# Four shifts of buffers and issue points in a two-layer streaming encoder: inputs loaded into query buffers, mixture stores, value differences and factor casts issued later

## The chip, the cores and the metric

The kernel runs on one core of one Trainium2 chip. The time is the device time of one execution in microseconds; the median of several executions is what counts. The engines are named as the profile names them: PE multiplies matrices (PEld loads its weights beside it), DVE, ACT and POOL work element by element, and SP issues nearly all DMAs, one after the other, in one queue.

## The reference, cut to what matters

One sequence of 2048 frames with 1024 channels goes through two layers, in float32.

```python
# layer 0: pooling mixer, then a gated embedding
h = rms_norm(x, a_norm);  u, z = split(h @ w_in, 2)
pooled = trailing_means(u, windows 2, 4, 8, 16) - u
x = x + (group_linear(pooled) * scale * silu(z)) @ w_out
x = x + (p[0] @ ple_w[0]) * sigmoid(x @ ple_gate_w[0])
# shared keys and values
k, v = split(rms_norm(x, kv_norm) @ w_kv, 2);  k = rms_norm(k by head, k_norm)
# layer 1: stick-breaking attention, 16 heads of 64
q, z = split(rms_norm(x, b_norm) @ w_in, 2);  q = rms_norm(q by head, b_q_norm)
a[t, s] = sigmoid(l[t, s]) * prod over s < j < t of (1 - sigmoid(l[t, j]))
x = x + ((a @ v) * silu(z)) @ w_out
x = x + (p[1] @ ple_w[1]) * sigmoid(x @ ple_gate_w[1])
```

## The kernel before

**Numbers in two parts.** Every float32 operand of PE is split into a rounded high part and the rest, its low part: ACT casts the high part, then DVE (or POOL) subtracts it from the source (`split`, L187 and L188 to L189; for weights `put_split`, L208 and L210 without a gain, L214 and L215 with one). A product takes three matmuls: high by high, high by low, low by high.

**Stages.** The sequence is cut into four chunks of 512 frames. `opening` runs layer 0 of chunk 0 (`mixed_part(0)`, `gated_part(0)`) and of chunk 1, and then `pair_part(0, 1)`, which makes keys, values, queries and gates of both chunks. `attend` then runs the attention of chunks 0 and 1, with the matmuls of layer 0 of chunks 2 and 3 interleaved (`beside_first`). `middle` does the gates of chunk 3 and `pair_part(2, 3)`; a second `attend` runs the attention of chunks 2 and 3 beside the end of layer 1; the last chunk's end comes alone.

**The pair.** `pair_part` multiplies a 2 by 2 block of activations (two chunks by two halves of the channels) with a 2 by 2 block of weights in seven products instead of eight (p1 to p7, 48 matmuls each, for each of the kinds v, k, q, z in the first pair and v, k, q in the second). The activation factors of p3 to p7 are differences, made by `build` on DVE and split; the weight factors of p4 to p7 are differences as well, made by `mixtures`: four weight tiles are loaded (L950), scaled by ACT (L970), subtracted by DVE (L976), and stored in `mixed`. The mixtures of k, q and v are made beside `gated_part(0)` and `mixed_part(1)`, one step every nine matmuls; those of z inside the first pair from its matmul 480 on, one step every six. `evacuate` takes the results out of PSUM (L993 on DVE, L997 on ACT) and hands them on; values go to `valued`, which makes a copy shifted by one frame by DMA (L752, L756) and has `differences` subtract it (L762), copy the high part (L765), make the low part (L766) and store both.

**Time inside the program.** A counter advances by one with every matmul. `after(n, do)` traces `do` n matmuls later and `store(n, ...)` a DMA to memory n matmuls later (L70). What is traced is then laid out by a scheduler with a simulated timeline of its own (`schedule_with_timeline_sim=True`): an instruction may stand earlier in its engine's queue than where it was traced, when its inputs are ready on that timeline, except where `tc.keep_in_program_order` pins it behind the instruction traced before it on its engine. In the pairs all matmuls are pinned; the loads of `mixtures` (L950) are pinned, and the loads of x in `prep` (L543) are pinned outside the attention.

**Buffers.** Raw weights (L225), x (L543), residuals and a few others share the ring `io` of four buffers; taking a buffer first settles the split of the tile that was there. The queries of the attention have the tag `q`, four buffers, which also hold the x of chunk 0 at the start (`load_first`) and, in the pairs, two split factors: the last one of p2 and the first one of p6 (`home`). `prep(1)` runs beside `gated_part(0)`, one tile of x every 22 matmuls; `prep(2)` in the last 140 matmuls of the first pair, one tile every 10; `prep(3)` beside the first attention. x is cast and split, and squared (L449, L452) for the norm; after the last reader its buffer is free.

**Weights** are planned in one list (`plan`); `pump` keeps up to nine units ahead of PE, and a unit is given back when its matmuls are done.

Of the kernel before, what the change touches and what calls it, by code (L numbers as in the profile page):

```python
# [10 lines left out]
F32 = mybir.dt.float32  # L11
F32R = mybir.dt.float32r
AF = mybir.ActivationFunctionType
ALU = mybir.AluOpType
# [18 lines left out]
def f(ap):  # L33
    return ap.bitcast(F32)


def half_of(pr, l):
    return pr[l] if isinstance(pr, tuple) else pr[:, l]
# [3 lines left out]
def trunk_kernel(ctx, tc, x, p, a_norm, wu_t, wz_a, w_group, a_scale, a_w_out, kv_norm, w_kv,  # L42
                 k_norm, b_norm, b_w_q, b_w_z, b_w_zs, b_q_norm, b_w_out, ple_a, ple_b, gate_a, gate_b, out):
    nc = tc.nc
    V, A, G = nc.vector, nc.scalar, nc.gpsimd
# [19 lines left out]
    def after(n, do):  # L65
        heapq.heappush(waiting, (time["now"] + n, time["seq"], do))
        time["seq"] += 1

    def store(n, **k):
        after(n, lambda: nc.sync.dma_start(**k))  # L70

    def late(n, *todo):

        def do():
            for op in todo:
                tc.keep_in_program_order(op())

        after(n, do)

    def pass_time(n=1):  # L80
        time["now"] += n
        while waiting and waiting[0][0] <= time["now"]:
            heapq.heappop(waiting)[2]()
# [44 lines left out]
    def scratch(name, shape):  # L128
        return dram.tile(shape, F32, name=name)
# [6 lines left out]
    vd = [[scratch(f"vd{s}_{b}", [8, P, 4, P]) for b in range(2)] for s in range(NSUB)]  # L136
# [5 lines left out]
    def flat(tag, bufs, dt=F32):  # L142
        return lambda nm, dt=dt: pool.tile([P, W5], dt, tag=tag, name=nm, bufs=bufs)
# [4 lines left out]
    def io(nm, owner=None):  # L148
        if ring[0] is not None:
            settle(ring[0])  # L150
        ring.append(owner)
        return io_(nm)
# [6 lines left out]
    qryt = flat("q", 4, F32R)  # L159
# [27 lines left out]
    def split(pr, src, lo, n=0):  # L187
        high = lambda: A.copy(out=half_of(pr, 0), in_=src)  # L188
        low = lambda: lo.tensor_tensor(out=half_of(pr, 1), in0=src, in1=f(half_of(pr, 0)), op=ALU.subtract)  # L189
        if n and not state["solo"]:  # L190
            late(n, high, low)
        else:
            high()
            low()
# [61 lines left out]
    def settle(pr):  # L256
        finish = unsplit.pop(id(pr), None)
        if finish:
            finish()
# [13 lines left out]
    def give_back():  # L273
# [10 lines left out]
    mixed = {(kind, name): scratch(f"mixed{kind}{name}", [P, 4, W5]) for kind in KINDS for name in PRODUCTS  # L284
             if name not in WHOLE and (kind != KINDS[0] or name not in READY)}
# [251 lines left out]
    def prep(s):  # L537
        ck = chunk[s]
        ck["x"] = []
        for o in range(KT):  # L540
            pr = pair("xp") if o < 7 else (row("xh", F32R), row("xl", F32R))
            xin = io("xin", pr)
            ins = nc.sync.dma_start(out=xin, in_=x[o * P : (o + 1) * P, s * W5 : (s + 1) * W5])  # L543
            ck["x"].append(pr)

            def finish(o=o, pr=pr, xin=xin):
                split(pr, xin, V if state["hold"] and state["solo"] else G)
                gather_squares(ck, "acc1", o, xin)

            if state["solo"]:  # L550
                tc.keep_in_program_order(ins)
            unsplit[id(pr)] = finish
            after(12 if state["solo"] else 20, lambda pr=pr: settle(pr))
            yield
        if not state["hold"]:
            pass_time(12)
            ck["rb1"] = bcast(token_norm(ck["acc1"], "x"), "x")
            return

        def total():  # L560
            ck["r1"] = token_norm(ck["acc1"], "x")

        def spread():
            ck["rb1"] = bcast(ck["r1"], "x")

        lag.append((time["now"] + 36, total))
        lag.append((time["now"] + 48, spread))
# [177 lines left out]
    def valued(s, b, j, vr):  # L745
        vs = tmp("vs")
        r0 = s * W5 + j * P
        store(6, out=vraw[b][r0 + P - 1 : r0 + P], in_=vr[P - 1 : P])

        def shifted():  # L750
            if r0:
                nc.sync.dma_start(out=vs[0:1], in_=vraw[b][r0 - 1 : r0])  # L752
            else:
                V.memset(vs[0:1], 0.0)
            for lo, hi in ((0, 112), (112, P - 1)):
                nc.sync.dma_start(out=vs[lo + 1 : hi + 1], in_=vr[lo:hi])  # L756

        after(10, shifted)
        after(38, lambda: differences(s, b, j, vr, vs))

    def differences(s, b, j, vr, vs):
        V.tensor_tensor(out=vs, in0=vs, in1=vr, op=ALU.subtract)  # L762
        vs = vs.rearrange("q (h d) -> q h d", d=HD)
        vv = t4("vv").rearrange("q l (h d) -> q (l h d)", d=HD).rearrange("q (h l d) -> q h l d", l=2, d=HD)
        after(4, lambda: A.copy(out=vv[:, :, 0, :], in_=vs))  # L765
        after(8, lambda: V.tensor_tensor(out=vv[:, :, 1, :], in0=vs, in1=f(vv[:, :, 0, :]), op=ALU.subtract))  # L766
        store(16, out=vd[s][b][:, :, j, :].rearrange("h q n -> q h n"),
              in_=f(vv).rearrange("q h e d -> q h (e d)"))

    def keyed(s, kind, b, j, qs):  # L770
# [110 lines left out]
    sets = {}  # L881
# [28 lines left out]
    def build(s):  # L910
        a11, a12 = sets["raw"][:4], sets["raw"][4:]
        rows, rb = chunk[s].pop("rows"), chunk[s]["rb2"]
        sets.pop("raw")
        for name in ("p3", "p5", "p7", "p6", "p4"):
            sets[name] = [home(8 + i) if name == "p6" and i < 3 else pair("xs") for i in range(4)]
        for i in range(4):
            V.tensor_tensor(out=rows[i][:, 1], in0=rows[i][:, 1], in1=rb, op=ALU.mult)
            split(sets["p5"][i], rows[i][:, 1], V)
        yield
        for i in range(4):  # L920
            V.tensor_tensor(out=rows[i][:, 0], in0=rows[i][:, 0], in1=rb, op=ALU.mult)
            V.tensor_tensor(out=rows[i][:, 0], in0=a11[i], in1=rows[i][:, 0], op=ALU.subtract)
            split(sets["p7"][i], rows[i][:, 0], V)
            yield
            V.tensor_tensor(out=a11[i], in0=rows[i][:, 1], in1=a11[i], op=ALU.subtract)
            split(sets["p6"][i], a11[i], V)
            yield
        for i in range(4):
            V.tensor_tensor(out=a12[i], in0=a12[i], in1=a11[i], op=ALU.subtract)
            split(sets["p3"][i], a12[i], V)  # L930
            yield
        for i in range(4):
            raw, scale = scaled(s, 4 + i, tmp)
            yield
            scale()
            split(sets["p4"][i], raw, V)
            yield

    def spare(n):
# [3 lines left out]
    def mixtures(kinds):  # L943
        todo = [(kind, i) for kind in kinds for i in range(4)]

        def load(kind, i):
            src, b0 = SOURCES[kind][0], 2 if kind == "v" else 0
            w = [spare(n) if kind == "z" else ppt("mx") for n in range(4)]
            for n, t in enumerate(w):
                tc.keep_in_program_order(nc.sync.dma_start(out=t, in_=src[b0 + n % 2][:, i + n // 2 * 4]))  # L950
            return w

        def put(kind, name, i, t):
            if kind == KINDS[0] and name in READY:
                pr = t4("mv")
                split(pr, t, V)
                d = once[kind, name, i] = scratch(f"mv{name}{i}", [P, 2, 1, W5])
                store(12, out=d.rearrange("q l k n -> q l (k n)"), in_=f(pr))
            else:
                store(12, out=mixed[kind, name][:, i], in_=t)  # L960

        w = None
        for n, (kind, i) in enumerate(todo):
            if w is None:
                w = load(kind, i)
                for _ in range(8):
                    yield
            for m, t in enumerate(w):
                kt = i + m // 2 * 4
                A.activation(out=t, in_=t, func=AF.Identity, scale=SOURCES[kind][1][:, kt : kt + 1])  # L970
            yield
            b11, b12, b21, b22 = w
            w = None
            for m, (name, a, b, c) in enumerate((("p5", b11, b12, b11), ("p7", b12, b22, b12),
                                                 ("p6", b22, b22, b11), ("p4", b21, b21, b22))):
                V.tensor_tensor(out=a, in0=b, in1=c, op=ALU.subtract)  # L976
                put(kind, name, i, a)
                if m == 0 and kind != "z" and n + 1 < len(todo):
                    w = load(*todo[n + 1])
                yield  # L980
            yield
            yield
# [458 lines left out]
```

## Time and profile before

| | us |
|---|---|
| median of three executions | 2677.32 |
| lowest and highest | 2673.27, 2681.02 |
| the profiled execution | 2670.83 |
| its span on the core | 2668.7 |
| granted share of PE's clock | 0.995 |

The profile is of one execution that is 6.5 us faster than the median. Idle time and waits below are taken from it. A row of waits gives who waited, for whom, the total in us, how often, and the longest one; a row of a window gives its bounds and length, the busy time of PE, PEld, DVE, ACT and POOL with their counts of instructions, the granted share of PE's clock, the busy share of the DMA engines and what they moved in GB/s. "SPq" is the DMA queue of SP.

### The profile page before, as it was taken

How to read it: one execution, taken by the hardware profiler on the slowest of the kernel's cores; microseconds unless marked ns; L12 is line 12 of the kernel's file. 1: busy time of each engine (PE TensorE's matmuls, PEld its weight loads, DVE VectorE, ACT ScalarE, POOL GpSimd, SP SyncE). 2: the span in 40 equal slices, each digit the busy share in tenths (PEclk: the TensorE clock that was granted, in tenths of full speed). 3: DMA queues.
4: the chain of work that ended last, by engine and by line, in shares of the span. 5: the costliest groups of instructions: out<-in, count | busy, mean ns of one | idle time of the engine just before them, and what ended most of it. 6: DMA issues, size and time to landing. Idle time of an engine off the chain costs nothing.

```text
span 2668.7 us, 38357 instructions
## 1 busy us (share of the span) xinstructions
PE 2620.7 (98%) x13070; PEld 2186.1 (82%) x13070; DVE 2035.1 (76%) x2812; ACT 1465.8 (55%) x2900; POOL 572.0 (21%) x470
## 2 busy tenths in 40 slices
PE   9999999999999999999999999999999999999999
PEld 7887888787788888888887888888888888888887
DVE  6746658776568887798677766889898999999842
ACT  5334335465557766555444675666665665556521
POOL 1214321143224325332310433110000100010000
PEclk9999999999999999999999999999999999999999
DMA  6799998877877898677868568765755574556554
GB/s 250 262 336 332 357 351 270 248 243 226 285 271 272 314 313 281 235 260 244 296 214 259 173 209 292 258 203 182 245 174 182 175 244 159 193 179 228 165 199 151
DMA packets 319551, 649.16 MB, mean 243 GB/s; under 512 B 48222, under 2 KB 87134, under 8 KB 319356
## 3 DMA queue, kind: packets, MB, share of 16 engines
q1 hardware_dynamic: 318780, 645.92, 71.7%
q8 instruction: 103, 1.69, 0.3%
q10 hardware_dynamic: 576, 0.79, 0.1%
q14 instruction: 92, 0.75, 0.1%
HBM read 464.66 MB, written 173.60 MB: 239 GB/s over the span
## 4 chain that ended last, share of the span: by engine, by line
PE 73%; DVE 12%; DMA 6%; ACT 3%; issue 3%; SPq 2%; POOL 1%; DVEq 0%; ACTq 0%; POOLq 0%
PE psd L51 38%; PE pso L51 8%; PE psl L51 8%; PE psa L55 7%; PE total L51 6%; PE own L51 5%; DVE pp L1231 3%; DVE at L1251 2%; DMA xin<-in_x_dram 1%; SPq L70 1%; POOL rq L181 1%; DMA vs<-qs 1%; DVE wpair L210 1%; PE pst L55 1%; DVE us L595 1%
## 5 line engine op out<-in xcount | busy, mean ns | idle before, releaser
L1231 DVE TENSOR_TENSOR_SCAN pp<-pp,floor 128x512 f32<-128x512 f32 (+3 forms) x640 | 725.3, 1169 | 10.8 <-ACT pp L1227 10.6
L1249 ACT CAST at<-psa 128x512 fp32r<-128x512 f32 (+3 forms) x640 | 302.5, 524 | 356.0 <-PE psa L55 354.2
L51 PE MATMUL psd<-x,wpair 128*128 128x512 f32 x1920 | 472.9, 391 | 0.0
L1251 DVE TENSOR_TENSOR at<-psa,at 128x512 fp32r<-128x512 f32 (+3 forms) x640 | 358.9, 599 | 122.6 <-ACT at L1249 120.2
L51 PEld LDWEIGHTS psd<-x,wpair 128*128 128x128 f32 x1920 | 358.8, 188 | 75.7 <-DMA wpair<-once 0.4
L51 PE MATMUL psd<-xp,wpair 128*128 128x512 f32 x1392 | 338.7, 392 | 0.3 <-DVE wpair L215 0.2
L51 PE MATMUL pso<-at,vv 128*128 128x512 f32 (+3 forms) x1280 | 318.9, 367 | 11.4 <-DVE at L1251 11.1
L1227 ACT ACTIVATE pp<-psl 128x512 f32<-128x512 f32 (+3 forms) x640 | 312.5, 549 | 7.5 <-PE psl L51 6.7
L51 PEld LDWEIGHTS psd<-xp,wpair 128*128 128x128 f32 x1392 | 258.5, 188 | 55.6 <-DVE wpair L215 1.1
L55 PE MATMUL psa<-ident,pp 128*128 128x128 f32 x2176 | 291.8, 274 | 0.0
L51 PEld LDWEIGHTS pso<-at,vv 128*128 128x128 f32 x1280 | 229.8, 188 | 72.3 <-DVE at L1251 26.8
L51 PE MATMUL total<-wpair,xs 128*128 128x512 f32 x1152 | 276.7, 396 | 6.3 <-DVE qs L993 4.1
L55 PEld LDWEIGHTS psa<-ident,pp 128*128 128x128 f32 x2176 | 252.9, 141 | 27.6
L51 PEld LDWEIGHTS total<-wpair,xs 128*128 128x128 f32 x1152 | 215.8, 189 | 53.6 <-DVE qs L993 4.5
L51 PE MATMUL psl<-kk,qa 128*128 128x512 f32 (+3 forms) x640 | 257.6, 407 | 0.0
L51 PE MATMUL psl<-kk,qb 128*128 128x512 f32 (+3 forms) x640 | 233.1, 364 | 2.4 <-ACT qb L1194 2.4
L51 PE MATMUL own<-wpair,xs 128*128 128x512 f32 x864 | 208.0, 396 | 4.8 <-ACT wpair L214 2.0
L51 PEld LDWEIGHTS own<-wpair,xs 128*128 128x128 f32 x864 | 161.5, 190 | 40.0 <-DVE wpair L215 2.8
L1279 POOL TENSOR_TENSOR os<-os,zt 128x512 f32<-128x512 f32 x32 | 52.2, 1632 | 638.9 <-ACT os L1278 618.8
L51 PE MATMUL psd<-og,wpair 128*128 128x512 f32 x744 | 185.2, 390 | 0.0
L51 PE MATMUL psd<-mp,wpair 128*128 128x512 f32 x768 | 179.9, 390 | 0.0
L51 PEld LDWEIGHTS psd<-mp,wpair 128*128 128x128 f32 x768 | 143.4, 188 | 29.9
(154 smaller groups left out, 3515.6 us busy)
## 6 DMA issues: line engine op xcount, KB each, us to landing
wpair<-once SPq DMA_DIRECT2D x322, 512.0 KB
kk<-kd SPq DMA_DIRECT2D x160, 256.0 KB
vv<-vd SPq DMA_DIRECT2D x160, 256.0 KB
once<-wpair SPq DMA_DIRECT2D x52, 512.0 KB
wpair<-wf SPq DMA_DIRECT2D x48, 512.0 KB
once<-kp SPq DMA_DIRECT2D x40, 512.0 KB
vd<-vv SPq DMA_DIRECT2D x32, 512.0 KB
kd<-hl SPq DMA_DIRECT2D x64, 256.0 KB
```

What stands on the lines that cost most here:

```text
L51: return held_in_order(nc.tensor.matmul(*a, **k))
L55: return held_in_order(nc.tensor.transpose(*a, **k))
L70: after(n, lambda: nc.sync.dma_start(**k))
L181: G.tensor_tensor(out=out_ap, in0=ms, in1=neghalf[:, 0:w], op=ALU.pow)
L210: (G if state["lo"] % state["every"] == 0 else V).tensor_tensor(out=pr[:, 1], in0=raw, in1=f(pr[:, 0]), op=ALU.subtract)
L595: V.tensor_tensor(out=us[:, lo:][:, ::-1], in0=cur[:, lo:][:, ::-1], in1=cur[:, lo - sh : n][:, ::-1], op=ALU.add)
L1227: A.activation(out=pp[:, r0:], in_=ps[:, :w], func=AF.Sigmoid, scale=-1.0)
L1231: V.tensor_tensor_scan(out=pp[:, r0:][:, ::-1], data0=pp[:, r0:][:, ::-1], data1=least, initial=1.0 if st["diag"] else st["carry"][j], op0 ...
L1249: A.copy(out=at[:, 0, cs], in_=pt[:, cs])
L1251: return lambda: V.tensor_tensor(out=at[:, 1, cs], in0=pt[:, cs], in1=f(at[:, 0, cs]), op=ALU.subtract)
L1279: G.tensor_tensor(out=os, in0=os, in1=zt, op=ALU.mult)
```

## The change

Five places are touched. In `prep` the tiles of x of chunks 1 and 2 are loaded into the four query buffers instead of the ring `io`, which also drops the settling of a ring tile there. Value differences are traced 44 instead of 38 matmuls behind their DMAs' start, their high copy 11 instead of 4 behind that, the low part 15 instead of 8, and the store 23 instead of 16. In `build` the split of every difference is traced five or six matmuls after the difference instead of at once. In `mixtures` the stores of the z mixtures are traced 20 instead of 12 matmuls behind, and the wait between the first loads and their use is 11 steps instead of 8.

```diff
@@ prep
-            xin = io("xin", pr)
+            xin = qryt("xin", F32) if s < 3 else io("xin", pr)
@@ valued
-        after(38, lambda: differences(s, b, j, vr, vs))
+        after(44, lambda: differences(s, b, j, vr, vs))
@@ differences
-        after(4, lambda: A.copy(out=vv[:, :, 0, :], in_=vs))
-        after(8, lambda: V.tensor_tensor(out=vv[:, :, 1, :], in0=vs, in1=f(vv[:, :, 0, :]), op=ALU.subtract))
-        store(16, out=vd[s][b][:, :, j, :].rearrange("h q n -> q h n"),
+        after(11, lambda: A.copy(out=vv[:, :, 0, :], in_=vs))
+        after(15, lambda: V.tensor_tensor(out=vv[:, :, 1, :], in0=vs, in1=f(vv[:, :, 0, :]), op=ALU.subtract))
+        store(23, out=vd[s][b][:, :, j, :].rearrange("h q n -> q h n"),
@@ build
-            split(sets["p5"][i], rows[i][:, 1], V)
+            after(6, lambda i=i: split(sets["p5"][i], rows[i][:, 1], V))
...
-            split(sets["p7"][i], rows[i][:, 0], V)
+            after(5, lambda i=i: split(sets["p7"][i], rows[i][:, 0], V))
...
-            split(sets["p6"][i], a11[i], V)
+            after(5, lambda i=i: split(sets["p6"][i], a11[i], V))
...
-            split(sets["p3"][i], a12[i], V)
+            after(5, lambda i=i: split(sets["p3"][i], a12[i], V))
...
-            split(sets["p4"][i], raw, V)
+            after(5, lambda i=i, raw=raw: split(sets["p4"][i], raw, V))
@@ mixtures
-                store(12, out=mixed[kind, name][:, i], in_=t)
+                store(20 if kind == "z" else 12, out=mixed[kind, name][:, i], in_=t)
...
-                for _ in range(8):
+                for _ in range(11):
                     yield
```

## The prediction

> **What bounds the kernel now.** First the head of the page, then the windows of the stages (first start to attention of chunks 0 and 1, that attention, gates and second pair, the second attention), then the chain that ended last.
>
> ```profile
> span 2668.7 us, 38357 instructions
> ```
>
> ```profile
> 8.00:785.00 777.00, 755.38 (x3476) 622.41 (x3477) 517.37 (x791) 377.30 (x673) 203.82 (x181) 0.99 0.84 288
> 785.00:1290.00 505.00, 499.18 (x2618) 421.41 (x2617) 426.24 (x572) 321.31 (x703) 174.75 (x140) 1.00 0.79 272
> 1290.00:1640.00 350.00, 346.56 (x1583) 284.76 (x1582) 233.92 (x351) 187.19 (x329) 102.55 (x88) 1.00 0.73 235
> 1640.00:2560.00 920.00, 910.28 (x4933) 769.73 (x4932) 830.30 (x1021) 561.40 (x1166) 82.15 (x51) 1.00 0.60 199
> ```
>
> ```profile
> 469.85 10.88 PE own L51 x48
> ```
>
> PE is the bound everywhere. Where it runs undisturbed it takes 10.88 / 48 = 0.227 us a matmul of 512 columns, and the change neither adds nor removes a matmul. So only PE's idle time can move: 777.0 - 755.4 = 21.6 us in the first row, where all five edits act, and 350.0 - 346.6 = 3.4 us in the third, where those in `differences` and `build` act again. To this comes PE time at a lowered clock behind the longer stalls. The waits of PE, asked window by window, say where it is (beside `gated_part(0)`; in the first pair around 515, 624 and 731 us; in the second pair):
>
> ```profile
> PE psd L51 <- DVE wpair L210: 2.9, 2, 2.1
> PE psd L51 <- ACT wpair L208: 2.2, 1, 2.2
> ```
>
> ```profile
> PE own L51 <- ACT wpair L214: 1.1, 1, 1.1
> PE own L51 <- DVE wpair L215: 0.7, 1, 0.7
> ```
>
> ```profile
> PE total L51 <- DVE qs L993: 4.1, 1, 4.1
> ```
>
> ```profile
> PE own L51 <- DVE qs L993: 2.8, 1, 2.8
> ```
>
> ```profile
> PE own L51 <- ACT qs L997: 1.2, 1, 1.2
> PE own L51 <- DVE wpair L215: 0.9, 1, 0.9
> PE own L51 <- ACT wpair L214: 0.9, 1, 0.9
> ```
>
> The windows around the three largest, with the granted clock in the column after POOL:
>
> ```profile
> 210.00:240.00 30.00, 24.89 (x105) 19.67 (x104) 21.16 (x22) 12.55 (x22) 14.93 (x10) 0.94 0.94 322
> 600.00:640.00 40.00, 34.03 (x150) 27.12 (x149) 25.45 (x41) 22.87 (x42) 11.61 (x10) 0.91 0.83 260
> 690.00:740.00 50.00, 45.69 (x199) 36.73 (x198) 23.39 (x37) 24.97 (x43) 0.00 (x0) 0.93 0.89 282
> ```
>
> The clock adds 0.06 x 30 = 1.8, 0.09 x 40 = 3.6 and 0.07 x 50 = 3.5 us to them.
>
> **How much a later trace point moves.** Four of the five edits only trace an instruction some matmuls later. Whether it moves on the chip is seen from two that the edits' kin made before:
>
> ```profile
> 425.94 0.48 DVE L754 MEMSET vs<- 1x512 f32 x1
> ```
>
> ```profile
> 437.05 1.29 PE L51 MATMUL own<-wpair,xs 128*128 128x512 f32 x5
> ```
>
> ```profile
> 544.78 0.69 DVE L976 TENSOR_TENSOR mz<-mz 128x512 f32<-128x512 f32 x1 [4.67 <-ACT mz L970]
> ```
>
> ```profile
> 545.50 0.32 SPq L70 DMA_DIRECT2D mixedzp<-mz  x1
> ```
>
> The memset of the first value tile is traced some 70 matmuls into the pair, yet it runs 11 us before p2, matmul 48, begins. The first z mixture's store, traced 12 matmuls (2.7 us) behind its subtraction, is issued 0.03 us after it. So a delay moves only what competes for a busy engine, and what is pinned. A pinned load traced later does go later.
>
> **The change part by part.**
>
> *x in query buffers, chunk 1.* Nothing is added: eight loads, casts, subtractions and squares as before. The raw gate weights get the ring `io` to themselves. SP's waits from 180 to 230 us show what the sharing cost:
>
> ```profile
> SPq L225 <- POOL xp L189: 2.5, 3, 0.8
> SPq L225 <- ACT sq L452: 2.0, 1, 2.0
> SPq L225 <- ACT acc L449: 0.5, 1, 0.5
> ```
>
> SP stood 5.0 us before raw weights because readers of x held the buffer, and what is behind stands too. PE then waits for the last weights of a group, the embedding's:
>
> ```profile
> 224.87 0.72 PE L51 MATMUL psd<-ple,wpair 128*128 128x512 f32 x2 [2.16 <-ACT wpair L208]
> ...
> 228.35 2.08 PE L51 MATMUL psd<-ple,wpair 128*128 128x512 f32 x4 [2.05 <-DVE wpair L210]
> ```
>
> With those 5.0 us back the weights come before they are needed: -(2.16 + 2.05 + 1.8) = -6.0. Bounds: 0, if the DMA engines are full anyway, and -6.9 with the first wait (2.9 - 2.05 = 0.9), which I leave since its weight stood in DVE's queue. The query buffers cannot be late here: a tile every 22 matmuls over four buffers leaves each 88 x 0.227 = 20 us.
>
> The Trainium skill says on its page "TensorE: Matmul & The Clock Gate", section "What's actually happening", that the clock halves after at least one idle window of about 3.4 us. Here two idle stretches of 2.2 and 2.1 us, with three matmuls between, stand beside a granted 0.94, so the row decides; by the page this term would be -4.2 and the sum below -7.8.
>
> *x in query buffers, chunk 2.* The same at the end of the first pair, but at one tile per 10 matmuls. PE has no wait there, so 0; what it can cost is the third case below.
>
> *z mixtures.* The stores stay where they are (the rows above). The wait of 11 steps for 8 moves the pinned loads of the next items: from matmuls 480, 570, 660, 750 to 480, 588, 696, 804. The fourth made the 4.1 us stall:
>
> ```profile
> 612.03 3.24 SPq L950 DMA_DIRECT2D mz<-in_b_w_z_dram  x4
> ```
>
> ```profile
> 617.62 0.72 ACT L970 ACTIVATE mz<-mz,gains 128x512 f32<-128x512 f32 x1 [5.67 <-DMA mz<-in_b_w_z_dram]
> ```
>
> ```profile
>   DMA mz<-in_b_w_z_dram: 15.9, 6
> ```
>
> ```profile
> PE pst L55 <- DVE qs L993: 0.9, 1, 0.9
> ```
>
> ACT stood 5.67 us on this load, with the squares, key casts and copies out of PSUM behind it, DVE behind those, and PE behind L993. There are six such waits (15.9 us of idle time before L970); the others cost PE at most the 0.9 us of the last row, at 547 us. 54 matmuls (12.2 us) later it falls between p6 and p3 of the queries, where DVE alone empties p3's banks. Ends: -(4.1 + 3.6) = -7.7 if it hurts nowhere, +7.7 if it hurts again and one of the two others moved does as well. I take half the gain, -3.9.
>
> *Mixtures of k, q, v.* The first wait shifts the chain by 3 x 9 matmuls, 6.1 us. Its end passes the end of `mixed_part(1)`, where the rest is run at once; those weights are used a whole `gated_part` later. 0, between -0.9 and +0.9, the first wait at 210 us.
>
> *Value differences.* In these stretches DVE stands for the shifted copies and with it L215, for which PE waits 0.7 and 0.9 us. The same room that lets instructions go early lets these, so of 1.6 I take -0.8; the ACT waits of 1.1 and 0.9 are for weights that land late and stay. The later stores feed the attention hundreds of matmuls on: 0.
>
> *Factor casts.* Both engines are crowded at the start of a pair; the casts give way to copies out of PSUM. At most the -1.2 of L997 in the second pair, at worst six matmuls, +1.4, if p5 comes late: 0.
>
> *New order.* Any change deals new waits of the size of those above; I add a middling one, +1.1.
>
> **Sum:** -6.0 - 3.9 - 0.8 + 1.1 = -9.6, on the profiled 2670.8 (its span and 2.1 us around it) 2661.2. The median shown is 6.5 higher, 2677.3, so 2667.7. What is late next is PE's wait at 731 us and the attention's own.
>
> **The rivals.**
>
> *The waits come again: 2676.* For it speak the early placement, the re-dealt z loads, and the DMA engines:
>
> ```profile
> 240.00:290.00 50.00, 50.00 (x229) 41.24 (x228) 34.70 (x48) 17.26 (x30) 17.86 (x21) 1.00 0.99 370
> ```
>
> They are 94% busy from 210 to 240 us and 99% after. If they limit there, raw weights issued earlier land no earlier than their bytes allow, and only -1 to -2 is left. Against it: the stretch before 210 us, into which loads would move, is freer (SP was waiting), and PE's waits end on ACT and DVE queues.
>
> The Trainium skill, "Trainium Kernel Development and Optimization", section "Key Constraints", has all queues share the same 16 engines and interleave; by that rule too moving a load's issue makes no bandwidth. The trace agrees as far as the 0.99 goes.
>
> *Slower: x waits for query buffers in SP's queue at the end of the first pair, 2687.* The hold of a buffer in `prep(2)`:
>
> ```profile
> L543 SPq DMA_DIRECT2D xin<-in_x_dram x8: 328/353/517, 736.2 to 756.0; - x8
> ...
> L189 DVE TENSOR_TENSOR xp<-xin,xp x7: 674/693/1381, 739.5 to 760.9; 128x512 fp32r<-128x512 f32 x7
> ...
> L189 DVE TENSOR_TENSOR xl<-xin,xh x1: 677/677/677, 762.0 to 762.0; 128x512 fp32r<-128x512 f32 x1
> ```
>
> ```profile
> 710.47 1.11 SPq L1188 DMA_DIRECT2D qa<-qd  x1
> ```
>
> First tile 736.2 to 740.2, last 756.0 to 762.7: 4.0 to 6.7 us, against a pace of 10 x 0.227 = 2.27. Four buffers (9.1 us) are enough, three (6.8) just. But the first query load already stood in this tag at 710.47, 60 us early; if it and its swapped copy keep two, each further tile is 6.5 - 4.5 = 2 us late, six of them 12. SP is held with the stores and the next stage's weights behind it; PE loses up to 12 and 3.5 of clock, +15.5, less the -6.0: +9.5. It decides from two buffers on. Against it: before, these loads waited for the ring as well,
>
> ```profile
> SPq L543 <- DVE wpair L210: 3.9, 4, 1.4
> ```
>
> and PE did not notice.
>
> **How the numbers follow.** Forecast (2661 to 2671) 0.47; waits come again (2671 to 2681) 0.33; slower (2681 to 2692) 0.15; all gains at once (-6.9 - 7.7 - 1.6 - 1.2 = -17.4, 2660, down to 2655 by the spread of the runs) 0.05. A measurement of this kernel tells about 0.3%, 8 us, from no change: 2669.3 and 2685.3 are the bounds. Faster: 0.85 of the first and the last, 0.45; slower: 0.15; same: 0.40. Range 2657 to 2685, which leaves out part of the last two.
>
> **What would show it.** Right: SP's raw weight loads no longer wait for readers of x from 180 to 230 us, PE's waits on the embedding's weights at 222 and 226 us are gone, the clock stays at 1.00 there, and the fourth z load costs PE less than 4 us. Wrong: those waits stand again, or L543 waits on x's own readers from 735 to 770 us with `wpair` loads behind it, or the first attention's start has a PE gap.

## The result and the profile after

| | us |
|---|---|
| before, median of six executions | 2675.15 (2672.75 to 2681.02) |
| after, median of six executions | 2659.64 (2651.94 to 2662.51) |
| after : before | 0.9936, 95% interval 0.9921 to 0.9952 |
| profiled execution, before and after | 2670.83 and 2658.17 |

The kernel became faster, by 15.5 us between the medians and by 0.64%, 17.1 us, by the ratio. The two profiled executions lie 12.7 us apart, so the traces show most of it, not all.

The head of the page after, and the windows of the same four stages as before (bounds and length; busy time of PE, PEld, DVE, ACT and POOL; granted clock; DMA share; GB/s):

```profile
span 2656.2 us, 38367 instructions
```

```profile
8.00:785.00 777.00, 762.58 (x3530) 630.06 (x3531) 527.48 (x806) 383.55 (x684) 205.45 (x183) 0.99 0.85 290
785.00:1290.00 505.00, 498.73 (x2621) 421.48 (x2621) 420.58 (x563) 318.73 (x697) 175.41 (x138) 1.00 0.80 275
1290.00:1640.00 350.00, 346.69 (x1597) 285.23 (x1595) 243.96 (x361) 194.81 (x345) 104.97 (x89) 1.00 0.74 237
1640.00:2560.00 920.00, 910.47 (x4915) 769.25 (x4916) 821.95 (x1012) 555.87 (x1154) 80.98 (x50) 1.00 0.60 197
```

PE's idle time in the first row is 777.0 - 762.6 = 14.4 us where it was 21.6; in the other rows it stayed (3.4 and 3.3 us in the third). Nearly all of the gain was made before 785 us. The waits of PE there, asked in three windows (180 to 250, 500 to 600 and 600 to 785 us), parted by dots:

```profile
PE pst L51 <- DVE acc L454: 1.7, 1, 1.7
...
PE pst L55 <- ACT hl L794: 4.0, 1, 4.0
PE total L51 <- ACT wpair L208: 0.5, 1, 0.5
...
PE own L51 <- DVE qs L993: 2.0, 2, 1.4
PE pst L55 <- ACT hl L794: 1.6, 2, 0.9
PE pst L51 <- DVE acc L454: 1.6, 1, 1.6
```

The waits for the embedding's weights (L210, L208) are gone, and so are those for L214 and L215 near 515 us; one of 0.5 us for L208 stands behind them, where it was 1.0. The 4.1 us at 624 us and the 2.8 us at 731 us for L993 have come down to 2.0 together. New are one wait of 4.0 us for the key casts, L794, and two short waits for the sum of squares, L454, in the norms of chunks 1 and 2. The windows around them, in the columns of the rows above:

```profile
210.00:240.00 30.00, 28.31 (x136) 23.37 (x135) 18.34 (x22) 10.79 (x22) 11.82 (x10) 1.00 0.92 329
530.00:560.00 30.00, 25.87 (x110) 20.68 (x109) 19.28 (x30) 18.23 (x32) 2.03 (x3) 0.89 0.89 297
600.00:640.00 40.00, 39.98 (x192) 32.88 (x191) 27.68 (x43) 27.04 (x49) 8.89 (x8) 1.00 0.74 217
690.00:740.00 50.00, 47.06 (x211) 38.05 (x210) 26.57 (x42) 26.41 (x47) 2.60 (x2) 1.00 0.87 277
740.00:770.00 30.00, 28.41 (x126) 23.05 (x124) 16.46 (x22) 15.58 (x28) 7.70 (x7) 0.94 0.88 302
```

The stall of the fourth z load (34.03 of 40 us busy, clock 0.91) is completely gone; in its place stands one at 545 us (25.87 of 30, clock 0.89).

The sharpest way to compare traces here is the start of the same matmul in each, since PE is busy nearly all the time. The table has the start of the first pair's matmul 0, 144, 480, 576, 816 and 1296, the start of that pair's last one and the end of the span: for before in us, then the difference of each profiled execution.

| | before | after | e1 x | e2 z | e3 values | e4 casts | e10 pin | e12 x and pin |
|---|---|---|---|---|---|---|---|---|
| matmul 0 | 423.7 | -5.8 | -7.4 | -1.6 | +1.8 | +1.9 | +2.5 | -8.2 |
| 144 | 458.8 | -5.1 | -7.5 | +5.3 | +1.8 | +1.9 | +2.5 | -8.2 |
| 480 | 539.6 | -8.2 | -7.1 | +5.1 | +0.1 | +2.7 | +3.5 | -7.2 |
| 576 | 564.4 | -2.1 | -7.7 | +11.1 | +0.5 | +2.0 | +2.4 | -8.3 |
| 816 | 633.9 | -11.2 | -8.8 | +3.5 | +2.1 | +2.4 | -5.8 | -17.5 |
| 1296 | 758.6 | -14.7 | -12.1 | 0.0 | -1.9 | +1.1 | -6.8 | -20.9 |
| last | 770.6 | -11.1 | -8.4 | +3.3 | +1.3 | +4.7 | -1.7 | -18.2 |
| span's end | 2668.7 | -12.4 | -5.1 | +3.2 | -2.5 | +2.4 | +1.0 | -15.3 |

Down the column of after: 5.8 us are won before the pair, 3.1 up to matmul 480 (where the value differences act; e3 alone wins 1.7 there), 6.1 lost at the new stall, 9.1 won up to matmul 816 (the old one), 3.5 won and 3.6 lost around the pair's end. e3 and e4 change nothing before matmul 0 and yet differ by 1.8 and 1.9 us there: one execution's marks are good to 2 or 3 us, and what is smaller is read from the timed ratios.

### The profile page after: what moved, and what is told of

Read it like the earlier page. It is cut to its first block, busy times and chain, and to the rows that moved or that the text cites. A ratio compares the mean times of both kernels' runs of the same rounds, so it can differ in the third digit from the quotient of the medians.

```text
span 2656.2 us, 38367 instructions
## 1 busy us (share of the span) xinstructions
PE 2615.9 (98%) x13070; PEld 2183.5 (82%) x13070; DVE 2036.9 (77%) x2812; ACT 1466.9 (55%) x2900; POOL 573.0 (22%) x470
## 4 chain that ended last, share of the span: by engine, by line
PE 78%; DVE 10%; DMA 6%; ACT 3%; issue 2%; SPq 1%; POOL 1%; DVEq 0%; ACTq 0%
PE psd L51 40%; PE pso L51 8%; PE psl L51 8%; PE psa L55 7%; PE total L51 7%; PE own L51 6%; DVE pp L1231 3%; DVE at L1251 2%; PE pst L55 1%; DMA xin<-in_x_dram 1%; DMA wraw<-in_w_kv_dram 1%; DVE us L595 1%; ACT at L1249 1%; SPq L70 1%; DMA wraw<-mixedzp 1%
## 5 line engine op out<-in xcount | busy, mean ns | idle before, releaser
L1231 DVE TENSOR_TENSOR_SCAN pp<-pp,floor 128x512 f32<-128x512 f32 (+3 forms) x640 | 726.9, 1172 | 11.1 <-ACT pp L1227 10.9
L51 PE MATMUL pso<-at,vv 128*128 128x512 f32 (+3 forms) x1280 | 318.6, 367 | 11.4 <-DVE at L1251 11.2
```

The costliest lines, as they stand in the source:

```text
L51: return held_in_order(nc.tensor.matmul(*a, **k))
L1231: V.tensor_tensor_scan(out=pp[:, r0:][:, ::-1], data0=pp[:, r0:][:, ::-1], data1=least, initial=1.0 if st["diag"] else st["carry"][j], op0 ...
```

## The experiments

All were timed in five rounds, beside the kernel before on the same chip; a ratio stands with its 95% interval. 0.1% is 2.7 us. Kernels of different groups, after among them, are compared through these ratios to before.

### The parts alone (e1 to e4)

e1, chunk 1's x alone:

```diff
-            xin = io("xin", pr)
+            xin = qryt("xin", F32) if s == 1 else io("xin", pr)
```

> Before, with one edit: x of chunk 1 alone goes into the query buffers. Theory (the raw weights get the ring back): PE's waits on the embedding's weights at 222 and 226 us go, the first pair's first matmul starts near 418 us instead of 423.7, and the whole time falls by 5 to 7 us (ratio about 0.998); behind the start of the pair nothing is worth more than 2 us. Rival (the engines of the DMA are full, and the gain came with the later mixtures): the pair starts at 422 to 424 us and the time stays within 2 us. Second rival (any edit deals the waits anew): the start may move, but the pairs move by several us as well.

Measured: 0.9966 [0.9955, 0.9977], -9.1 us. The window of 180 to 240 us of before, after and e1, in that order:

```profile
180.00:240.00 60.00, 54.89 (x237) 44.46 (x237) 40.33 (x45) 30.90 (x55) 26.76 (x18) 0.97 0.92 326
```

```profile
180.00:240.00 60.00, 58.31 (x268) 48.23 (x267) 41.44 (x49) 33.07 (x61) 30.33 (x22) 1.00 0.97 363
```

```profile
180.00:240.00 60.00, 60.00 (x277) 49.98 (x276) 42.58 (x51) 34.72 (x63) 27.96 (x20) 1.00 1.00 372
```

PE goes from 54.9 us of 60 to 60.0, at full clock, and the DMA engines move 372 GB/s where they moved 326: they were not full, they were waiting for SP. By the rows of its waits, SP's from 180 to 230 us add up to nearly the same in the three traces (27.4, 27.5 and 28.1 us), but they are of another kind: for engines they were 23.8 us in before, 11.3 in after and 8.2 in e1; for other transfers 3.6, 16.2 and 19.9. In SP's waits of after, from 180 to 230 us, no reader of x is named any more (L225 is the load of raw weights):

```profile
SPq L669 <- DVE wpair L210: 4.0, 3, 1.9
SPq L70 <- DVE mx L976: 2.8, 3, 1.3
SPq L225 <- DMA once<-wpair: 2.6, 3, 0.9
...
SPq L225 <- DVE wpair L210: 1.8, 3, 1.4
```

What SP waits for now are ring buffers that raw weights hold until their split (L210; L669 loads a residual into the same ring), earlier stores, and the data of its own stores (L70). By its marks e1 wins 7.4 us before the pair; the window of before had 60 - 54.9 = 5.1 us of idle time and 0.03 x 60 = 1.8 us of clock to give, 6.9. After wins less, 5.8, since PE waits 1.7 us for L454 there, which e1 does not. The 9.1 us of the ratio are more than the 5 to 7 that were expected. Where the rest is won isn't told: behind the pair's start e1's marks swing between -12.1 and -5.1 us.

e2, both edits in `mixtures`:

```diff
-                store(12, out=mixed[kind, name][:, i], in_=t)
+                store(20 if kind == "z" else 12, out=mixed[kind, name][:, i], in_=t)
...
-                for _ in range(8):
+                for _ in range(11):
```

> Before, with the two edits of mixtures alone (z stores traced 20 behind, 11 steps of waiting). Theory: the last z load is issued some 35 us earlier in the first pair than before (188 us behind the pair's start), so PE's wait of 4.1 us behind L993 and its half clock go, -7; an earlier z load then meets the key casts and may give up to 6 back near matmul 540. Sum -1 to -7, all of it inside the first pair. Rival (the delay moves the loads later, as the prediction had it): the last load is issued 190 to 200 us behind the pair's start and the wait is halved at most. Second rival (the later mixtures of k, q, v made the gain ahead of the pair): the pair starts at 418 us.

Measured: 0.9997 [0.9986, 1.0008], nothing, where 1 to 7 us were expected. The table shows why: -7.6 us from matmul 576 to 816 besides +6.0 from 480 to 576, the same two swings as in after, and +6.9 between 0 and 144. That last one is a wait of PE at the start of the pair (418 to 432 us), with the clock at 0.77 behind it, 0.23 x 22 = 5 us:

```profile
PE total L51 <- ACT wpair L214: 2.5, 2, 1.4
```

```profile
418.00:440.00 22.00, 19.38 (x69) 14.78 (x68) 11.43 (x18) 7.47 (x13) 1.21 (x2) 0.77 0.64 224
```

Ahead of the pair e2 shows something else. Its x is still in the ring, and yet most of the 5.1 us for the embedding's weights is gone, while the wait for L454 is there (180 to 250 us):

```profile
PE pst L51 <- DVE acc L454: 1.4, 1, 1.4
PE psd L51 <- DVE wpair L210: 0.6, 1, 0.6
PE psd L51 <- ACT wpair L208: 0.5, 1, 0.5
```

So the later mixtures of k, q and v shorten these waits too, for a gain of only 1.6 us at matmul 0; e7 below, with the wait of 11 steps alone, has 1.6 us for L454 and begins the pair 2.1 us earlier. In after both edits act on the same waits, and what each is worth there beside the other isn't shown.

e3, the value differences, their copies and stores later:

```diff
-        after(38, lambda: differences(s, b, j, vr, vs))
+        after(44, lambda: differences(s, b, j, vr, vs))
...
-        after(4, lambda: A.copy(out=vv[:, :, 0, :], in_=vs))
+        after(11, lambda: A.copy(out=vv[:, :, 0, :], in_=vs))
```

(and 8 to 15, 16 to 23, as in the change)

> Before, with the later value differences alone. Theory: DVE no longer stands for the shifted copies ahead of L215, so the matmuls 384 to 480 of both pairs lose 1 to 2.5 us each of their waits; the whole is 2 to 4 us faster. Rival (a later trace point does not move what is early anyway): the order of DVE changes little in these stretches, PE's waits at 515 and 1453 us stand, and the time stays within 2 us.

Measured: 0.9990 [0.9981, 1.0000], -2.7 us, at the edge of what can be told. What DVE stood before L762, in before, after and e3 (us, times):

```profile
  DMA vs<-qs: 13.9, 10
```

```profile
  DMA vs<-qs: 2.4, 5
```

```profile
  DMA vs<-qs: 3.9, 6
```

The edit does what its steps say: ten waits for the shifted copies, 13.9 us of DVE's time, become five or six. In the first pair PE's waits near 515 us shrink with it, from 1.8 to 1.0 us; in the second pair they stand (for L214 and L215 together 1.8 us before, 2.2 in e3), so the gain that was expected in both pairs is seen in one.

e4, the five splits in `build` five or six matmuls later, as in the change:

```diff
-            split(sets["p5"][i], rows[i][:, 1], V)
+            after(6, lambda i=i: split(sets["p5"][i], rows[i][:, 1], V))
```

> Before, with the later casts of the product factors alone. Theory: only the first 150 matmuls of each pair change, where ACT and DVE are crowded; PE's wait for L997 at 1389 us shrinks by 0.5 to 1.2 us, nothing else; time within 2 us. Rival (any edit deals the waits anew): the first pair moves by more than 3 us somewhere behind matmul 400, which no factor cast stands near.

Measured: 1.0001 [0.9992, 1.0009], nothing by the ratio. Its trace loses 3.6 us at the end of the first pair, behind matmul 1296, where a wait for L454 comes in that before has not, and PE's wait for L997 in the second pair fell from 1.2 us to this:

```profile
PE own L51 <- ACT qs L997: 0.2, 1, 0.2
```

The four ratios add up to -0.46%, after has -0.64%. The intervals of five ratios (each some 0.1 wide to a side) cover the difference of 0.18, so no extra gain of the parts in company is shown. One candidate is seen in the table: e2's 6.9 us after matmul 0 are not in after, where they are +0.7.

### What of the x edit it is (e5, e6)

e5 loads chunk 1's x into query buffers, but still settles the split in the ring's oldest place for every tile, as `io` did:

```diff
+            if s == 1:
+                if ring[0] is not None:
+                    settle(ring[0])
+                ring.append(pr)
-            xin = io("xin", pr)
+            xin = qryt("xin", F32) if s == 1 else io("xin", pr)
```

> Before, with x of chunk 1 in the query buffers, but each of its eight tiles still settles the raw weight that was fourth last and takes a place in the list of owners, as before. Only the buffers are freed, the traced splits stay as early as they were. Theory (the raw weights' loads waited for buffers that x held): the pair starts at 416 to 418 us as with x moved outright, the time is 7 to 10 us below before. Rival (what helped is that splits are no longer traced early): at least half of the 7.4 us ahead of the pair is lost, the pair starts at 420 us or later.

Measured: 0.9957 [0.9943, 0.9971], -11.5 us, no less than e1. Its pair starts at 416.6 us, as expected. It is the buffers, not the settling that fell away with them.

e6 is after with chunk 2's x back in the ring:

```diff
-            xin = qryt("xin", F32) if s < 3 else io("xin", pr)
+            xin = qryt("xin", F32) if s == 1 else io("xin", pr)
```

> After, with x of chunk 2 back in the ring. Theory (x of chunk 2 was never on the path): within 2 us of after, that is 13 to 17 below before. Rival (query buffers hold SP's queue at the end of the pair, the third case of the prediction): 3 to 6 us faster than after, and PE's wait for DVE's L454 before the attention goes. Second rival (the ring held the weights of p4 there as well): 3 to 6 us slower than after, with more PE idle time between matmuls 1200 and 1344 of the pair.

Measured: 0.9938 [0.9925, 0.9952] beside after's 0.9936: no worth of chunk 2's buffers is shown, within some 4 us to a side. Nor is a cost. In after, SP's waits for x from 725 to 765 us, and its first load of a query for the attention:

```profile
SPq L543 <- ACT wpair L208: 0.3, 1, 0.3
SPq L543 <- ACT xp L188: 0.2, 1, 0.2
```

```profile
746.23 0.40 SPq L1188 DMA_DIRECT2D qa<-qd  x1
```

The first query load, which before stood in a buffer of that tag at 710.47 us, is issued 36 us later: it gives way to x, so x does not wait for it.

### The two halves of the z edit (e7, e8)

e7 has the wait of 11 steps alone, e8 the later z stores alone:

```diff
-                for _ in range(8):
+                for _ in range(11):
```

> Before, with only the wait of 11 steps. Theory: the chain of k, q, v mixtures ends later, so raw weights of the first pair meet it and PE waits for L214 near the pair's start, with the half clock (+5 to +7 there); the z loads go early and the wait behind L993 at 624 us goes (-7). Sum -2 to +2. Rival (the wait at the pair's start comes from the z stores): no such wait here, and 4 to 7 us faster.

```diff
-                store(12, out=mixed[kind, name][:, i], in_=t)
+                store(20 if kind == "z" else 12, out=mixed[kind, name][:, i], in_=t)
```

> Before, with only the z mixtures' stores traced 20 matmuls behind. Theory: the loads are pinned behind the DMA traced before them; with the store traced behind the next load they are no longer pinned to it, float early, and the fourth is issued at least 15 us earlier than before; the wait at 624 us shrinks or goes, -3 to -7 in all, and nothing changes ahead of the pair. Rival (the stores run early anyway, so the later trace point changes nothing): within 1 us, and the fourth load stands where it stood.

Measured: e7 0.9990 [0.9980, 1.0001], e8 0.9979 [0.9970, 0.9989], -2.7 and -5.6 us. What the prediction had otherwise is when the sixteen z loads are issued, from the first to the last start (durations in ns, lowest, median, highest, stand ahead of the starts). Before, after, e7 and e8, in that order:

```profile
L950 SPq DMA_DIRECT2D mz<-in_b_w_z_dram x16: 327/437/1326, 539.1 to 614.8; - x16
```

```profile
L950 SPq DMA_DIRECT2D mz<-in_b_w_z_dram x16: 328/422/954, 531.6 to 578.0; - x16
```

```profile
L950 SPq DMA_DIRECT2D mz<-in_b_w_z_dram x16: 328/426/852, 538.9 to 587.3; - x16
```

```profile
L950 SPq DMA_DIRECT2D mz<-in_b_w_z_dram x16: 328/432/1300, 539.0 to 595.2; - x16
```

Each edit traces something later, and each brings the last load 20 to 37 us **earlier** (21 to 31 us, counted from the pair's start). The pin of L950 holds it behind the DMA traced just before it; where that one is a store that the scheduler may itself lay out early, the load goes with it. (That this is how it comes about is argued from the code; the times are shown.) Once earlier, the loads make ACT stand in another place, with other work behind. In e8 ACT stands 4.62 us on one, a key cast follows, and PE waits for it (ACT at 592 us, then PE's waits from 575 to 640 us):

```profile
592.15 0.72 ACT L970 ACTIVATE mz<-mz,gains 128x512 f32<-128x512 f32 x1 [4.62 <-DMA mz<-in_b_w_z_dram]
```

```profile
PE pst L55 <- ACT hl L794: 3.9, 2, 3.0
```

e7 has e2's wait for L214 at the start of the pair, 2.5 us, which e8 has not.

### ACT before the z load: the scaling pinned (e9 to e11)

If the harm is that ACT's queue reaches the scaling L970 before its load has landed, then pinning L970 takes it away without a word on the loads. e10 does so in before, e9 in after; e11 pins L762 in e9 as well.

```diff
-                A.activation(out=t, in_=t, func=AF.Identity, scale=SOURCES[kind][1][:, kt : kt + 1])
+                ins = A.activation(out=t, in_=t, func=AF.Identity, scale=SOURCES[kind][1][:, kt : kt + 1])
+                if kind == "z":
+                    tc.keep_in_program_order(ins)
```

```diff
-        V.tensor_tensor(out=vs, in0=vs, in1=vr, op=ALU.subtract)
+        tc.keep_in_program_order(V.tensor_tensor(out=vs, in0=vs, in1=vr, op=ALU.subtract))
```

> After, with ACT's scaling of the z mixtures (L970) pinned behind what is traced before it on ACT, so that it comes at its traced place, 11 steps or 66 matmuls behind its loads, and not at the place where the simulated timeline has the loads landed. Theory (PE's wait for the key casts at 544 us, 4.0 us and a half clock, is ACT standing on a z load ahead of them): ACT's idle time before L970 falls from 9.2 us to under 2, the wait at 544 us goes, and the time falls by another 3 to 7 us below after. Rival (ACT is late there for its own amount of work, or for the stores of key tiles): the wait stays at 3 us or more and the time within 2 us of after.

> Before, with the same pin alone. Theory (the wait of 4.1 us behind L993 at 624 us came from ACT standing 5.7 us on the fourth z load): that wait goes, ACT stands under 2 us before L970, the first pair is 4 to 8 us shorter from matmul 768 to 816, and the time is 4 to 8 us below before. Rival (the first pair's queue of SP is what is late, and ACT would stand for the next thing): PE's wait moves by some matmuls and the time is within 2 us of before.

> After, with the pin on the z scaling and a second pin on DVE: the value differences (L762) come at their traced place, 44 matmuls behind the values. Theory (DVE stands for the shifted copies because the differences run early): DVE's idle time before L762 falls to under 3 us from 13.9 before, PE's waits near matmul 384 to 480 of both pairs shrink by another 1 us each, and the time is 1 to 3 us below the run with the first pin alone. Rival (what PE waits for there is raw weights that land late): within 1.5 us of the run with the first pin alone.

Measured: e10 0.9967 [0.9955, 0.9979], -8.8 us; e9 0.9939 [0.9924, 0.9953] and e11 0.9947 [0.9932, 0.9963], both where after stands without a pin. ACT's idle time before L970 on the z loads was 15.9 us before and is 9.2 after:

```profile
  DMA mz<-in_b_w_z_dram: 9.2, 7
```

With the pin no such row is left in e9, e10 or e12. The loads themselves move as well, though no edit names them: the last one starts at 621.0 us in e10 (614.8 before) and at 625.1 in e9 (578.0 in after). Before, the pin was worth a third of a per cent. (The traced execution of e10, 2671.49 us, is 7.5 us above its median and shows little of that. Up to matmul 816 its pair is 8.3 us shorter than before's, by the marks at 0 and 816; then PE waits 3.4 us for L995, the copy that is L993 in before, at 639 us.) After, no gain of the same pin is shown: the wait at 545 us is gone, but ACT, freed of the z loads, stands in another place, and PE's waits for key casts are as long in all, 5.8 us where they were 5.6 (e9, the timeline of ACT at 594 us, the idle time in brackets, and PE's waits from 500 to 785 us):

```profile
594.39 0.60 ACT L794 ACTIVATE hl<-pst 128x512 f32<-128x512 f32 x1 [4.92 <-DMA kd<-hl]
```

```profile
PE pst L55 <- ACT hl L794: 5.8, 3, 3.1
```

Here L794 stands itself, 4.92 us, until the store of an earlier key tile has freed its buffer. In e11 DVE's idle time before L762, 2.4 us in after, is gone as well, and no gain over e9 is shown.

### The two that carry (e12)

e12 has only chunk 1's x in query buffers and the pinned scaling; nothing else of the change.

> Before, with two edits: x of chunk 1 in the query buffers, and the z scaling pinned on ACT. Theory (the change is made of two gains at two places, the raw weights beside the first gate and ACT's wait on z loads, and the rest of it is small): they add, 9.1 + 8.2 = 17 us below before, ratio 0.993 to 0.995, level with after. Rival (the gains overlap, since the pair's queues are late anyway): no more than 11 us below before.

Measured: 0.9935 [0.9921, 0.9948], median 2655.07 us (2652.88 to 2655.81) beside 2672.07. The two parts add up (0.34% and 0.33% alone, 0.65% together), and two short edits do as much as the five of the change; against after it is not shown to be faster. PE's waits from 500 to 785 us:

```profile
PE pst L51 <- DVE acc L454: 1.8, 1, 1.8
PE pst L55 <- ACT hl L794: 1.7, 2, 1.0
PE own L51 <- DVE qs L995: 1.4, 2, 1.2
PE own L51 <- ACT wpair L214: 1.4, 1, 1.4
```

Neither the old stall at 624 us nor the new one at 545 us is there.

## Why the prediction came out as it did

The time fell, as forecast, and lies in the range; it fell by more, 15.5 to 17.1 us for 9.6. The median, 2659.6, is where the prediction put "all gains at once", 2660, but not for that case's reasons: the gain of the z mixtures was largely spent again, and x alone gave more than its bound. Landing there is chance. Step by step:

- **x, chunk 1: mechanism right, size too small.** SP's waits, the embedding's weights and the clock from 210 to 240 us went as described; the pair began 5.8 us earlier in after, for -6.0. That these agree is chance, since the 5.8 holds a new wait of 1.7 us for L454 and the later mixtures work on the same waits (e2). Alone it wins 7.4 us before the pair (e1), a little more than the bound of 6.9, and 9.1 to 11.5 us by the ratios of e1 and e5: the first of the two waits for L210, left out of the sum because its weight stood in DVE's queue, went too. (The "three matmuls" between the two idle stretches of PE were five, two at 224.87 and three at 225.44 us.)
- **x, chunk 2: right**, nothing that shows (e6).
- **z mixtures: this step failed.** It said "A pinned load traced later does go later", and placed the fourth load 54 matmuls on, between p6 and p3. It went the other way, from 612.0 to 571.3 us at its first issue, 35 us earlier counted from the pair's start. The stall at 624 us went in full, as under the better end, and a second one came, 4.0 us and 0.11 x 30 = 3.3 us of clock at 545 us, because ACT stands 4.26 us on the second load with a key cast behind it (SP's queue, then ACT, in after):

```profile
571.34 1.42 SPq L950 DMA_DIRECT2D mz<-in_b_w_z_dram  x2
```

```profile
546.15 1.33 ACT L970 ACTIVATE mz<-mz,gains 128x512 f32<-128x512 f32 x2 [4.26 <-DMA mz<-in_b_w_z_dram]
547.39 0.57 ACT L794 ACTIVATE hl<-pst 128x512 f32<-128x512 f32 x1
```

  Before, ACT stood as long on the first z load (4.08 us, at 543 us), and PE waited 0.9: the price of such a stand is set by what is behind it. From matmul 480 to 816 after wins 3.0 us, so -3.9 was near by luck, as the difference of two larger swings. Also wrong was that the later stores do nothing: with them alone the last z load starts 20 us earlier (e8), and e8 is the only half with an interval clear of 1.
- **Mixtures of k, q, v: 0 expected.** In e2 and e7 the wait of 11 steps goes with 2.5 us for L214 at the start of the pair, more than the bound of 0.9; in after this wait isn't there. Nothing at this place in after, then, but the step had no word of it. Nor had it that the shift shortens the waits for the embedding's weights and brings the wait for L454 near 230 us (e2 and e7; e1 and e8 have none there).
- **Value differences: right in kind, small.** -0.8 for some -2.7 (e3, its interval from -5.1 to 0). The waits for L214 and L215 near 515 us, 1.8 us, are gone in after and 1.0 in e3. In the second pair e3 did not shorten them, though after did (to 0.8 us).
- **Factor casts: right**, 0 (e4).
- **New order, +1.1:** new waits came as said, the 1.7 and 1.6 us for L454. But the second is not peculiar to the change: between 745 and 770 us it stands in the trace of every kernel here but before. The wait at 731 us, named as late next, fell from 2.8 to 2.0 us, in two parts, and the clock stayed at 1.00. The table shows both, -3.5 and +3.6; they cancel.
- **"The waits come again", full DMA engines: fell.** The share rose from 0.92 to 1.00 in e1 (0.97 in after) as soon as SP issued earlier, so 0.92 was the effect of the waits, not their cause. Half of that rival came true elsewhere, in the z loads.
- **"Slower", x waits for query buffers: fell** (e6, and the query load at 746 us).

Beside its first term the prediction weighed a rule on the clock against a row; rows of after bear on it too. Behind the 1.6 us for L454 the clock falls (in steps of 3.41 us):

```profile
751.57:754.98 3.41, 2.37 (x14) 2.13 (x15) 2.87 (x5) 2.71 (x6) 0.49 (x1) 1.00 0.89 313
754.98:758.39 3.41, 3.41 (x12) 2.71 (x10) 0.79 (x2) 1.22 (x2) 1.17 (x2) 0.50 1.02 386
758.39:761.80 3.41, 3.41 (x17) 2.84 (x16) 0.52 (x1) 2.34 (x4) 0.00 (x0) 1.00 0.95 327
```

That is 0.50 x 3.41 = 1.7 us lost behind 1.6 us of idle time, and PE was busy for 2.37 of the 3.41 us ahead of the fall. The Trainium skill ("TensorE: Matmul & The Clock Gate", section "What's actually happening") asks for an idle window of about 3.4 us; the trace does not agree.

Two things stay open. How much the z edits are worth beside the other edits wasn't measured by a kernel that lacks only them. And why the 6.9 us that e2 loses at the start of the pair are not lost in after was not tried; that x was earlier there is a guess.

## What to carry to other kernels

A load that can wait for its buffer should not share a ring with loads that PE needs soon: the queue issues in order, and its 5 us of standing here lay beside DMA engines that were 92% busy and looked nearly full. Where a scheduler moves instructions by a timeline of its own, "trace it later" is no handle on a load; look in the trace where it went, and pin the instruction that would stand in an engine's queue, rather than the transfer that it waits for (worth 0.33% in before, nothing that shows in after). Before a stall is counted as won, ask what the same engine will stand on next: ACT had three such places for one.

## What the hardware showed unexpectedly

The granted clock fell behind idle times of PE of only 1.6 us (0.50 for 3.41 us, from 754.98 us in after), which doubles the price of such a wait. Length alone does not decide it: the 1.7 us for the same kind of instruction at 228 us in after and the 1.4 us at 721 us left the clock at 1.00 (windows 210 to 240 and 690 to 740 us). What else decides was not tried, but the traces narrow it. In all fourteen, every change of the clock lies on a grid of 3.41 us, the same through one trace, and a fall is to 0.50, for one to three steps while the kernel runs: 3.41 us at 755 us in after, 6.83 at 547 us, 10.24 at 427 us in e2. In the step of after ahead of the fall at 755 us six matmuls of 512 columns begin (and eight of a single one); in the steps in which PE idled at 228 and 721 us nine of 512 begin in each, where 15 are usual:

```profile
225.92:229.33 3.41, 2.24 (x10) 1.50 (x9) 0.90 (x1) 2.16 (x5) 1.46 (x2) 1.00 1.04 405
717.44:720.85 3.41, 2.34 (x11) 1.60 (x9) 3.40 (x6) 1.75 (x3) 0.00 (x0) 1.00 1.02 384
```

Counted over all fourteen traces from 200 to 785 us, each step at full clock with four or fewer such matmuls is followed by a fall, none with eight or more is, and those with five to seven are followed by one in some cases. So it looks as if the work done in a step counts, and a wait that straddles two steps can leave the clock alone; this is read from the traces, not tried by an experiment.
